# A chunked RWKV-7 recurrence in a hybrid decoder step: chunks of 64 tokens in place of 32, whole-array products, triangles inverted by blocks of 32

## The chip, the cores and the metric

The kernel runs on one core of a Trainium2 chip. The metric is the device time of one execution in microseconds (us). Before the change the median of three runs is 1478.64 us (1477.01 to 1479.61).

## What is computed

One layer of a hybrid decoder for 512 prompt tokens and 8 x 4 sample tokens, all in float32. A pre-RMSNorm and one large input projection (`w_in`, 1024 to 9472 columns) feed three branches (a gMLP gate, an RWKV-7 recurrence, a cross-attention to 256 memory tokens); three branch projections, an output projection and a squared-ReLU MLP follow. The part that is changed is the recurrence, for 16 heads of width 64, over the 512 prompt tokens:

```
def step(S, inp):                      # per token, S is [value, key]
    r_t, w_t, k_t, v_t, a_t, b_t = inp
    sa = einsum('bhij,bhj->bhi', S, a_t)
    S = S * w_t[:, :, None, :] + sa[..., None] * b_t[:, :, None, :] + v_t[..., None] * k_t[:, :, None, :]
    return S, einsum('bhij,bhj->bhi', S, r_t)
```

The kernel does not go token by token. It cuts the prompt into chunks, and inside a chunk the rule is solved by products with a triangular matrix and its inverse; only the state S goes from chunk to chunk.

## The kernel before, in words

**The trunk.** All projections are 128x128 weight tiles against 544 tokens (`trunk`, L490 to L520; the products are at L500). Each weight is split into a high and a low fp32r part (L198 on ScalarE, L211 on VectorE), so a tile costs three products of two column ranges (256 and 288). A "trunk product" below is one of these. The input projection has 74 columns of tiles, 3552 products in all (their inputs are named `hh` and `hl`).

**The streams.** Everything else is a set of generators (`Stream`), which a planner interleaves with the trunk: `build` first runs `body` dry, with a model of each engine's costs (`Model`, L102), notes which stream went next, and then emits the instructions in that order. So each engine's order is fixed, and TensorE, which runs in order, stands still when the next product's input is late. Between the pieces of the other streams the planner puts trunk products; what is left of the input projection after the recurrence's stage runs in the next stage (gate, attention).

**The recurrence's streams** (heads in pairs, two pairs make a group `g`, four groups):
- `prep_pair` (L823): decays, normalised keys, then the Gram products of a pair (L919, L921: 64x64 tiles of the array, 16 chunks), masked by VectorE into `CT`, `A2` (L929 to L935).
- `inv_stream` (L993): for a group, 32 unit triangles of 32x32 are inverted side by side on GpSimd, 30 steps of two instructions (L1007, L1009), with VectorE transposes around (L1002, L1014, L1016), then 64 products of 32x32 tiles (L1021).
- `fill` (L962): the keys are transposed by TensorE (L973, 128 columns to 64 rows) into `Em`, the values by VectorE into `Xe`, `Xo`.
- `chain_stream` (L1044): the serial part. For each of 16 chunks three steps, each a round trip TensorE to ScalarE or VectorE and back: L1063 and L1065 (state and in-chunk inputs), L1079 (the inverse), L1090 and L1092 (the new state). A step is four float32 products in tiles of the array (64x64, 96x64 or 128x64); for TensorE a float32 product is two recorded passes, so a step has eight.
- `out_stream` (L1125), `sample_stream` (L1166): norm and gate of the recurrence's output, and the sample tokens.

In the stage after, `gate_in` (L1413) and `layer_norm` prepare the gate, whose weights `sgw` are loaded and masked (L1469, recorded at L439), and `gate_out` (L1493) uses them.

## Time and profile before

| | us |
|---|---|
| median of three runs | 1478.64 |
| the profiled execution | 1483.1 |
| its span in the profile | 1481.1 |
| TensorE (PE) busy | 1396.5 (94%) |
| VectorE (DVE) busy | 906.7 (61%) |
| ScalarE (ACT) busy | 588.1 (40%) |
| GpSimd (POOL) busy | 396.1 (27%) |

The trace gives each instruction with start, duration, source line, shape and what ended the wait ahead of it. Matmuls are pipelined: a product's own duration (some 0.2 to 0.3 us) is longer than the distance to the next one, so costs on TensorE are read from start to start. In a timeline row `x8` means eight recorded instructions in a row of that kind.

### The profile page before, as it was taken

To read this page: it belongs to the slowest core of one execution; us is meant where nothing else is said; L and a number is where in the kernel's file an instruction comes from. 1 tells how busy PE (TensorE), PEld (TensorE's weight loads), DVE (VectorE), ACT (ScalarE), POOL (GpSimd) and SP (SyncE) were. 2 spreads that over 40 slices of the span, in tenths; PEclk is the share of its full clock that TensorE was granted. 3 is DMA by queue.
4 is the path that set the end of the run, shared out by engine and by line. 5 is a ranking of instruction groups with operands and counts; after the bars stand their busy time and mean duration, and the time that the engine had idled before them with its cause. 6 is when DMAs were issued, how large, how long until landed. Compare 5 with 4: busy or idle time off the path is not lost.

```text
span 1481.1 us, 30854 instructions
## 1 busy us (share of the span) xinstructions
PE 1396.5 (94%) x12340; PEld 1300.1 (88%) x12340; DVE 906.7 (61%) x1570; ACT 588.1 (40%) x1460; POOL 396.1 (27%) x466
## 2 busy tenths in 40 slices
PE   7899979999998899899979999999999999999996
PEld 7799978888878798777879997789999999999996
DVE  5758878848878787686647443344664454444544
ACT  3434326655654466455332222222333423323222
POOL 5320380533047107302234210122100030120213
PEclk9999989989999999899999999999999999999998
DMA  6642312213212323343583677544423222323222
GB/s 219 176 137 84 91 51 78 64 59 100 85 48 84 100 88 98 98 132 116 177 289 113 211 262 245 196 155 134 134 81 95 91 86 86 94 83 95 88 86 82
DMA packets 101888, 177.41 MB, mean 120 GB/s; under 512 B 14929, under 2 KB 28497, under 8 KB 101745
## 3 DMA queue, kind: packets, MB, share of 16 engines
q1 hardware_dynamic: 99904, 172.06, 36.9%
q8 instruction: 97, 1.59, 0.5%
q0 software_dynamic: 640, 2.23, 0.4%
q10 hardware_dynamic: 1200, 1.16, 0.2%
q14 instruction: 47, 0.38, 0.1%
HBM read 147.89 MB, written 27.51 MB: 118 GB/s over the span
## 4 chain that ended last, share of the span: by engine, by line
PE 66%; DVE 11%; POOL 10%; issue 5%; DMA 4%; ACT 3%; SPq 0%; POOLq 0%; DVEq 0%; ACTq 0%
PE pst L500 54%; POOL Xinv L1009 4%; POOL Tt L1007 4%; DVE wlo L211 2%; PE pst L1645 1%; PE pst L1678 1%; PE pst L545 1%; DMA wraw<-memk 1%; PE psc L1079 1%; POOL gn_va L1122 1%; PE psc L1063 1%; PE pst L1021 1%; PE psc L1090 1%; DMA gv<-zv_d 1%; PE pst L1816 1%
## 5 line engine op out<-in xcount | busy, mean ns | idle before, releaser
L211 DVE TENSOR_TENSOR wlo<-wraw,whi 128x512 fp32r<-128x512 f32 x372 | 309.6, 851 | 62.1 <-ACT whi L198 59.9
L198 ACT CAST whi<-wraw 128x512 fp32r<-128x512 f32 x372 | 223.4, 618 | 184.1 <-PE pst L500 103.3
L500 PE MATMUL pst<-hh,whi 128*128 128x256 f32 (+1 forms) x1184 | 258.5, 300 | 5.7 <-DVE y_f L1154 1.9
L500 PE MATMUL pst<-hh,wlo 128*128 128x256 f32 (+1 forms) x1184 | 258.6, 300 | 4.1 <-DVE wlo L211 4.1
L500 PE MATMUL pst<-hl,whi 128*128 128x256 f32 (+1 forms) x1184 | 255.6, 298 | 0.0
L500 PEld LDWEIGHTS pst<-hh,whi 128*128 128x128 f32 x1184 | 192.6, 193 | 13.4 <-issue 2.5
L500 PEld LDWEIGHTS pst<-hh,wlo 128*128 128x128 f32 x1184 | 192.4, 192 | 10.7 <-DVE wlo L211 4.6
L500 PEld LDWEIGHTS pst<-hl,whi 128*128 128x128 f32 x1184 | 193.4, 192 | 5.1 <-issue 1.8
L1784 POOL TENSOR_TENSOR x<-x,dn 128x544 f32<-128x544 f32 x24 | 41.7, 1737 | 293.1 <-DVE dn L1782 293.1
L500 PE MATMUL pst<-gh,whi 128*128 128x256 f32 (+1 forms) x512 | 106.2, 289 | 0.0
L500 PE MATMUL pst<-gl,whi 128*128 128x256 f32 (+1 forms) x512 | 105.5, 287 | 0.0
L500 PE MATMUL pst<-gh,wlo 128*128 128x256 f32 (+1 forms) x512 | 105.2, 288 | 0.0
L1086 ACT COPY YU<-psc 32x64 f32<-32x64 f32 x256 | 51.8, 202 | 81.1 <-DVE Xe L1083 76.9
L1007 POOL TENSOR_TENSOR Tt<-Xinv 128x30 f32<-128x30 f32 (+14 forms) x120 | 66.6, 555 | 64.9 <-DVE Xinv L1002 56.0
L500 PE MATMUL pst<-y_h,whi 128*128 128x256 f32 (+1 forms) x384 | 80.9, 292 | 2.8 <-DVE sp L1499 2.3
L500 PEld LDWEIGHTS pst<-gl,whi 128*128 128x128 f32 x512 | 82.7, 189 | 0.0
L500 PEld LDWEIGHTS pst<-gh,wlo 128*128 128x128 f32 x512 | 81.8, 188 | 0.3 <-DVE wlo L211 0.3
L500 PEld LDWEIGHTS pst<-gh,whi 128*128 128x128 f32 x512 | 81.9, 188 | 0.1
L500 PE MATMUL pst<-y_l,whi 128*128 128x256 f32 (+1 forms) x384 | 80.4, 290 | 0.0
L500 PE MATMUL pst<-y_h,wlo 128*128 128x256 f32 (+1 forms) x384 | 79.9, 290 | 0.0
L500 PE MATMUL pst<-mh,whi 128*128 128x256 f32 (+1 forms) x256 | 65.1, 295 | 10.6 <-ACT whi L198 10.6
L1009 POOL TENSOR_TENSOR Xinv<-Xinv,Tt 128x30 f32<-128x30 f32 (+14 forms) x120 | 72.4, 604 | 9.4
(401 smaller groups left out, 2895.8 us busy)
## 6 DMA issues: line engine op xcount, KB each, us to landing
wraw<-win SPq DMA_DIRECT2D x148, 256.0 KB, 2.9
wraw<-up SPq DMA_DIRECT2D x64, 256.0 KB, 2.9
wraw<-down SPq DMA_DIRECT2D x64, 256.0 KB, 2.9
wraw<-br SPq DMA_DIRECT2D x48, 256.0 KB, 3.6
craw<-ck SPq DMA_DIRECT2D x16, 512.0 KB, 5.4
craw<-cv SPq DMA_DIRECT2D x16, 512.0 KB, 4.4
gz_d<-gzs SPq DMA_DIRECT2D x24, 272.0 KB, 3.6
gt<-gz_d SPq DMA_DIRECT2D x24, 272.0 KB, 2.8
```

Of the source, the lines that this page charges most:

```text
L198: self.nc.scalar.copy(hi, raw)
L211: (self.nc.gpsimd if pool else self.nc.vector).tensor_tensor(lo, raw, hi, op=ALU.subtract)
L500: PE.matmul(ps[:, o:o + n], lhsT=w[:, c], rhs=x[kt][:, s:s + n], start=kt == 0 and i == 0, stop=kt == KT - 1 and i == 2)
L545: PE.matmul(ps[:, o:o + n], lhsT=lhsT, rhs=rhs[:, s:s + n], start=True, stop=True)
L1007: G.tensor_tensor(t3, X[:, j + 1:32, j:j + 1].to_broadcast([128, n, j]), X[:, j:j + 1, 0:j].to_broadcast([128, n, j]), op=ALU.mult)
L1009: G.tensor_tensor(X[:, j + 1:32, 0:j], X[:, j + 1:32, 0:j], t3, op=ALU.add)
L1021: PE.matmul(ps[q:q + 32, m * 32:m * 32 + 32], lhsT=Tt[q:q + 32, m, :], rhs=CT[q:q + 32, m, 0:32], start=True, stop=True, tile_position=(q, q))
L1063: PE.matmul(ps[64:128, pi * 64:pi * 64 + 64], lhsT=Ae[0:96, pi, c, :], rhs=Xe[0:96, pi, c, :], start=True, stop=True, tile_position=(0, 64))
L1079: PE.matmul(ps[q:q + 64, pi * 64:pi * 64 + 64], lhsT=CT[q:q + 64, m, :], rhs=Wt[q:q + 64, pi, :], start=True, stop=True, tile_position=(q, q))
L1086: S.copy(YU[q + 32 * pi:q + 32 * pi + 32, c, :], p3[q:q + 32, pi, :])
L1090: PE.matmul(ps[0:64, pi * 64:pi * 64 + 64], lhsT=Em[64:128, pi, c, :], rhs=Xe[64:128, pi, c, :], start=True, stop=True, tile_position=(64, 0))
L1784: G.tensor_tensor(x1[j], x1[j], t, op=ALU.add)
```

## The change

A chunk has 64 tokens, and there are 8 of them instead of 16 (`CH`, `NCH`). The three steps of a chunk are now products over the whole array (128x64, four of them, in steps one and three; 128x128, two, in step two), without a tile position; of the result one half of the rows is used for each head. The Gram products of a pair are 16 of 64 rows by 128 columns instead of 32 of 64x64, and TensorE's transposes in `fill` are 64 of 128x128 instead of 128 of 128x64. A 64x64 unit triangle is inverted as two 32x32 blocks (the same 30 steps on GpSimd, for 32 blocks side by side) and an off-diagonal block, which takes two sets of 32 products of 32x32, and a third set of 32 products of 64x64 then applies the inverse, in place of one set of 64 products of 32x32. The evacuations of a chunk are spread over ScalarE and VectorE.

```diff
@@ -21,7 +21,7 @@
-CH = 32
+CH = 64
 NCH = TP // CH
...
+    Wts = [sb(rp, [128, 2, 2, 64], f"Wt{i}") for i in range(2)]
...
-            PE.matmul(ps[64:128, o:o + 64], lhsT=BK[0:64, c, :], rhs=A2[0][0:64, pi, c, :],
-                      start=True, stop=True, tile_position=(0, 64))
-            PE.matmul(ps[0:64, o:o + 64], lhsT=BK[64:128, c, :], rhs=A2[1][64:128, pi, c, :],
-                      start=True, stop=True, tile_position=(64, 0))
...
+            ps, sl = yield from take()
+            for i in range(4):
+                for e in range(2):
+                    o = e * 512 + i * 128
+                    PE.matmul(ps[:, o:o + 128], lhsT=BK[64 * e:64 * e + 64, 4 * h + i, :],
+                              rhs=A2[e][64 * e:64 * e + 64, pi, 4 * h + i, :], start=True, stop=True)
+            yield DONE
+            p4 = ps.rearrange("p (e c t) -> p e c t", e=2, t=128)
+            for e in range(2):
+                q, n = 64 * e, 64 - 64 * e
+                m = mk[:, n:n + 128].unsqueeze(1).to_broadcast([128, 4, 128])
+                V.tensor_tensor(CT[q:q + 64, ms, :], p4[64:128, e], m[64:128], op=ALU.mult)
+                V.tensor_tensor(A2[e][n:n + 64, pi, cs, :], p4[0:64, e], m[0:64], op=ALU.mult)
+                yield DONE
...
-            for c in range(c8, c8 + 8):
-                PE.transpose(ps[0:64, (c - c8) * 128:(c - c8) * 128 + 128], BK[:, c, :], ident)
+            for i in range(4):
+                PE.transpose(ps[:, i * 128:i * 128 + 128], BK[:, 4 * half + i, :], ident)
             for n in range(2):
-                V.transpose(Xe[64:96, pi, cs, n * 32:n * 32 + 32],
-                            v[n * 32:n * 32 + 32, tsl].rearrange("p (c t) -> p c t", t=CH))
-                V.transpose(Xo[0:32, pi, cs, n * 32:n * 32 + 32],
-                            v[64 + n * 32:96 + n * 32, tsl].rearrange("p (c t) -> p c t", t=CH))
-            yield DONE
-            p3 = ps[0:64].rearrange("p (c t) -> p c t", t=128)
-            S.copy(Em[0:64, pi, c8:c8 + 8, :], p3[:, :, 64:128])
-            V.tensor_copy(Em[64:128, pi, c8:c8 + 8, :], p3[:, :, 0:64])
+                for th in range(2):
+                    for X, q, r in ((Xe, 64, 0), (Xo, 0, 64)):
+                        V.transpose(X[q + 32 * th:q + 32 * th + 32, pi, cs, n * 32:n * 32 + 32],
+                                    v[r + n * 32:r + n * 32 + 32, tsl].rearrange(
+                                        "p (c t) -> p c t", t=CH)[:, :, 32 * th:32 * th + 32])
+            yield DONE
+            p3 = ps[:, 0:512].rearrange("p (c t) -> p c t", t=128)
+            S.copy(Em[:, pi, cs, 64:128], p3[:, :, 64:128])
+            S.copy(Em[0:64, pi, cs, 0:64], p3[64:128, :, 0:64])
+            V.tensor_copy(Em[64:128, pi, cs, 0:64], p3[0:64, :, 0:64])
...
-            V.transpose(X, CT[:, :, 32:64].rearrange("p m t -> p t m"))
+            for q in (0, 64):
+                V.transpose(X[q:q + 64].rearrange("p t (m h) -> p t m h", h=2),
+                            CT[q:q + 64, :, q:q + 64].rearrange("p m (h t) -> p t m h", h=2))
...
+                G.memset(T4[q:q + 32, :, 1, :], 0.0)
+                for h in range(2):
+                    r = slice(q + 32 * h, q + 32 * h + 32)
+                    G.tensor_copy(CT[r, :, r], TT4[r, :, h, :])
+            yield DONE
+
+            O1 = X[:, 0:16, :]
+            ps, sl = yield from take()
+            for m in range(2 * NCH):
+                for q in (0, 64):
+                    PE.matmul(ps[q + 32:q + 64, m * 32:m * 32 + 32], lhsT=CT[q:q + 32, m, q + 32:q + 64],
+                              rhs=T4[q:q + 32, m, 0, :], start=True, stop=True, tile_position=(q, q + 32))
+            p3 = ps[:, 0:512].rearrange("p (m t) -> p m t", t=32)
+            S.copy(O1[32:64], p3[32:64])
+            V.tensor_copy(O1[96:128], p3[96:128])
+            pt_free(sl)
             yield DONE
             ps, sl = yield from take()
             for m in range(2 * NCH):
                 for q in (32, 96):
-                    PE.matmul(ps[q:q + 32, m * 32:m * 32 + 32], lhsT=Tt[q:q + 32, m, :],
-                              rhs=CT[q:q + 32, m, 0:32], start=True, stop=True, tile_position=(q, q))
-            for pi in range(2):
-                for q in (32, 96):
-                    S.copy(CT[q:q + 32, pi * NCH:pi * NCH + NCH, 0:32],
-                           ps[q:q + 32, pi * 512:pi * 512 + 512].rearrange("p (c t) -> p c t", t=32))
+                    PE.matmul(ps[q:q + 32, m * 32:m * 32 + 32], lhsT=TT4[q:q + 32, m, 1, :],
+                              rhs=O1[q:q + 32, m, :], start=True, stop=True, tile_position=(q, q))
+            p3 = ps[:, 0:512].rearrange("p (m t) -> p m t", t=32)
+            S.copy(T4[32:64, :, 0, :], p3[32:64])
+            V.tensor_copy(T4[96:128, :, 0, :], p3[96:128])
+            pt_free(sl)
+            for q in (0, 64):
+                V.transpose(CT[q:q + 32, :, q + 32:q + 64], T4[q + 32:q + 64, :, 0, :])
+            yield DONE
+            ps, sl = yield from take()
+            for m in range(2 * NCH):
+                for q in (0, 64):
+                    PE.matmul(ps[q:q + 64, m * 64:m * 64 + 64],
+                              lhsT=Tt[q:q + 64, 2 * m:2 * m + 2, :].rearrange("p h t -> p (h t)"),
+                              rhs=CT[q:q + 64, m, 64 - q:128 - q], start=True, stop=True, tile_position=(q, q))
+            p3 = ps.rearrange("p (m t) -> p m t", t=64)
+            S.copy(CT[0:64, :, 64:128], p3[0:64])
+            V.tensor_copy(CT[64:128, :, 0:64], p3[64:128])
...
-                    PE.matmul(ps[64:128, pi * 64:pi * 64 + 64], lhsT=Ae[0:96, pi, c, :], rhs=Xe[0:96, pi, c, :],
-                              start=True, stop=True, tile_position=(0, 64))
-                    PE.matmul(ps[0:64, pi * 64:pi * 64 + 64], lhsT=Ao[:, pi, c, :], rhs=Xo[:, pi, c, :],
-                              start=True, stop=True, tile_position=(0, 0))
-                Wt = sb(rp, [128, 2, 64], "Wt", bufs=2)
-                S.copy(Wt, ps[:, 0:128].rearrange("p (a b) -> p a b", b=64))
+                    for e, (A, X) in enumerate(((Ae, Xe), (Ao, Xo))):
+                        o = pi * 128 + e * 64
+                        PE.matmul(ps[:, o:o + 64], lhsT=A[:, pi, c, :], rhs=X[:, pi, c, :],
+                                  start=True, stop=True)
+                p3 = ps[:, 0:256].rearrange("p (a b) -> p a b", b=128)
+                Wt = Wts[c % 2]
+                S.copy(Wt[0:64, :, 0, :], p3[0:64, :, 0:64])
+                V.tensor_copy(Wt[64:128, :, 1, :], p3[64:128, :, 64:128])
+                S.copy(YU[64:128, :, c, :], p3[64:128, :, 0:64])
+                S.copy(YU[0:64, :, c, :], p3[0:64, :, 64:128])
...
-                    m = pi * NCH + c
-                    for q in (0, 64):
-                        PE.matmul(ps[q:q + 64, pi * 64:pi * 64 + 64], lhsT=CT[q:q + 64, m, :], rhs=Wt[q:q + 64, pi, :],
-                                  start=True, stop=True, tile_position=(q, q))
-                p3 = ps[:, 0:128].rearrange("p (a b) -> p a b", b=64)
-                V.tensor_copy(Xo[32:64, :, c, :], p3[32:64])
-                V.tensor_copy(Xe[96:128, :, c, :], p3[96:128])
-                for pi in range(2):
-                    for q in (0, 64):
-                        S.copy(YU[q + 32 * pi:q + 32 * pi + 32, c, :], p3[q:q + 32, pi, :])
+                    PE.matmul(ps[:, 256 + pi * 128:384 + pi * 128], lhsT=CT[:, pi * NCH + c, :],
+                              rhs=Wt[:, pi].rearrange("p a b -> p (a b)"), start=True, stop=True)
+                p4 = ps[:, 256:512].rearrange("p (a b) -> p a b", b=128)
+                V.tensor_copy(Xe[0:64, :, c, :], p4[0:64, :, 0:64])
+                S.copy(Xo[64:128, :, c, :], p4[64:128, :, 64:128])
+                V.tensor_tensor(YU[64:128, :, c, :], YU[64:128, :, c, :], p4[64:128, :, 0:64], op=ALU.add)
+                V.tensor_tensor(YU[0:64, :, c, :], YU[0:64, :, c, :], p4[0:64, :, 64:128], op=ALU.add)
...
-                    PE.matmul(ps[0:64, pi * 64:pi * 64 + 64], lhsT=Em[64:128, pi, c, :], rhs=Xe[64:128, pi, c, :],
-                              start=True, stop=True, tile_position=(64, 0))
-                    PE.matmul(ps[64:128, pi * 64:pi * 64 + 64], lhsT=Em[0:64, pi, c, :], rhs=Xo[0:64, pi, c, :],
-                              start=True, stop=True, tile_position=(0, 64))
-                p3 = ps[:, 0:128].rearrange("p (a b) -> p a b", b=64)
-                for A, rows in ((Xe, slice(0, 64)), (Xo, slice(64, 128))):
+                    for e, X in enumerate((Xe, Xo)):
+                        o = pi * 128 + e * 64
+                        PE.matmul(ps[:, o:o + 64], lhsT=Em[:, pi, c, :], rhs=X[:, pi, c, :], start=True, stop=True)
...```

Here is TensorE's order around two chain steps of the first group. `psc` is the PSUM tile of a chain step, `Xe` and `Xo` hold state and inputs of the even and the odd head, `AG0e` and `AG0o` the masked Gram products, `CT` the inverse. Before:

```order
L1063 MATMUL psc<-Xe,AG0e 64x64
L1065 MATMUL psc<-Xo,AG0o 64x64
L1063 MATMUL psc<-Xe,AG0e 64x64
L1065 MATMUL psc<-Xo,AG0o 64x64
L500 MATMUL pst<-hh_97,whi 128x256
L500 MATMUL pst<-hh_97,whi 128x288
...
L1079 MATMUL psc<-Wt,CT_1027 64x64 x4
```

The first two steps, with the changed kernel:

```order
L1093 MATMUL psc<-Xe,AG0e 128x64
L1093 MATMUL psc<-Xo,AG0o 128x64
L1093 MATMUL psc<-Xe,AG0e 128x64
L1093 MATMUL psc<-Xo,AG0o 128x64
L500 MATMUL pst<-hl_101,whi 128x256
L500 MATMUL pst<-hl_101,whi 128x288
...
L1108 MATMUL psc<-Wt_1034,CT_1029 128x128 x2
```

In the whole order there were 192 such steps, 135 of which stood alone between trunk products; now there are 96, of which 61 stand alone.

TensorE's order at the first inversion (`Tt` is the inverted block, transposed; `Xinv` the work tile). Before:

```order
L500 MATMUL pst<-hh_93,whi 128x256
L500 MATMUL pst<-hh_93,whi 128x288
L1021 MATMUL pst<-CT_1027,Tt 32x32 x64
L500 MATMUL pst<-hl_101,whi 128x256
```

The same place in the changed kernel:

```order
L500 MATMUL pst<-hh_93,whi 128x288
L1027 MATMUL pst<-Tt,CT_1029 32x32 x32
L500 MATMUL pst<-hl_101,whi 128x256
...
L500 MATMUL pst<-hh_95,wlo 128x288
L1037 MATMUL pst<-Xinv,TT 32x32 x32
L500 MATMUL pst<-hh_96,whi 128x256
...
L500 MATMUL pst<-hh_92,whi 128x288
L1049 MATMUL pst<-CT_1029,Tt 64x64 x32
```

Between the Gram products of pair 1 and the first product of the inversion there were 282 trunk products; now there are 348. Between the first product of `gate_in` and the first of `gate_out`, in the stage after, there were 410; now there are 294. From `gate_out` on, TensorE's order is the same in both kernels.

## Rows read from the trace of the kernel before

**Rows 1.** The page, part 1: busy time of each engine.
```profile
PE 1396.5 (94%) x12340; PEld 1300.1 (88%) x12340; DVE 906.7 (61%) x1570; ACT 588.1 (40%) x1460; POOL 396.1 (27%) x466
```
**Rows 2.** Windows: stretch, length, busy us by engine, granted clock, DMA share, GB/s.
```profile
82.00:755.00 673.00, 633.05 (x6380) 567.16 (x6380) 501.69 (x983) 337.88 (x992) 231.41 (x311) 0.96 0.31 95
```
**Rows 3.** Waits of TensorE from 105 to 755: us in total, times, longest.
```profile
PE psc L1090 <- DVE Xe L1083: 11.5, 10, 3.1
PE pst L1021 <- DVE Tt L1014: 7.1, 1, 7.1
PE psc L1063 <- DVE Xe L1098: 3.3, 3, 1.3
```
**Rows 4.** Timeline of TensorE around a chain step: start, duration.
```profile
247.04 0.41 PE L500 MATMUL pst<-hl,whi 128*128 128x256 f32 x2
247.29 0.41 PE L500 MATMUL pst<-hh,wlo 128*128 128x256 f32 x2
247.63 0.27 PE L1063 MATMUL psc<-Xe,AG0e 96*64 96x64 f32 x1
...
247.86 0.22 PE L1065 MATMUL psc<-Xo,AG0o 128*64 128x64 f32 x1
...
248.37 0.41 PE L500 MATMUL pst<-hl,whi 128*128 128x256 f32 x2
```
**Rows 5.** Groups by line, TensorE: the second chain step's recorded passes.
```profile
L1079 PE MATMUL psc<-Wt,CT 64*64 64x64 f32 x512 | 28.9, 232 | 0.0
```
**Rows 6.** Timeline of TensorE: whole-array passes of 2 columns, then trunk.
```profile
231.61 1.17 PE L858 MATMUL pst<-bones,t_x 128*128 128x2 f32 x10
232.64 0.50 PE L500 MATMUL pst<-hl,whi 128*128 128x256 f32 x2
232.97 0.41 PE L500 MATMUL pst<-hh,wlo 128*128 128x256 f32 x2
```
**Rows 7.** Timeline of TensorE: whole-array passes of 128 and 32 columns, then trunk.
```profile
831.92 1.05 PE L1493 MATMUL pst<-sgw,vn 128*128 128x128 f32 x8
832.81 0.31 PE L1494 MATMUL pst<-sgs,vn 128*128 128x32 f32 x2
832.95 0.49 PE L500 MATMUL pst<-y_l,whi 128*128 128x256 f32 x2
```
**Rows 8.** Groups by line: the trunk's weight loads (PEld).
```profile
L500 PEld LDWEIGHTS pst<-hh,whi 128*128 128x128 f32 x1184 | 192.6, 193 | 13.4 <-issue 2.5
```
**Rows 9.** Timeline of TensorE: two products in tiles of 64 rows.
```profile
229.06 0.38 PE L845 MATMUL pst<-la,wa 64*128 64x256 f32 x1
229.07 0.38 PE L846 MATMUL pst<-la,wa 64*128 64x256 f32 x1
229.28 0.40 PE L845 MATMUL pst<-la,wa 64*128 64x288 f32 x1
```
**Rows 10.** Timeline of TensorE: the Gram products of pair 0, first pass and trunk after.
```profile
124.19 0.27 PE L919 MATMUL pst<-AG0e,BK 64*64 64x64 f32 x1
...
126.21 0.52 PE L500 MATMUL pst<-hl,whi 128*128 128x256 f32 x2
```
**Rows 11.** Timeline of TensorE: eight transposes of `fill`, then trunk.
```profile
180.18 1.03 PE L973 MATMUL pst<-ident,BK 128*64 128x128 f32 x8
180.97 0.49 PE L500 MATMUL pst<-hh,whi 128*128 128x256 f32 x2
```
**Rows 12.** Timeline of TensorE: products of the first inversion, and of the third.
```profile
220.04 3.62 PE L1021 MATMUL pst<-CT,Tt 32*32 32x32 f32 x128 [7.14 <-DVE Tt L1014]
...
489.37 2.21 PE L1021 MATMUL pst<-CT,Tt 32*32 32x32 f32 x128
```
**Rows 13.** Groups by line, VectorE: the transpose ahead of an inversion.
```profile
L1002 DVE STREAM_TRANSPOSE Xinv<-CT 128x1024 f32<-128x1024 f32 x4 | 7.9, 1980 | 0.1
```
**Rows 14.** Timeline: the gate's weights masked on GpSimd, and their first product.
```profile
816.42 1.10 POOL L439 TENSOR_SCALAR_AFFINE_SELECT sgw<-sgw 128x1024 f32<-128x1024 f32 x1 [6.33 <-issue]
...
829.55 1.05 PE L1493 MATMUL pst<-sgw,vn 128*128 128x128 f32 x8
```

More of the change, by code (lines that the diff above doesn't have):

```diff
@@ L705, in body @@
     vb_d = dp.tile([8, 128, TP], F32, name="vb_d")
-    for i in range(2):
-        G.memset(AG[i][1][32:64], 0.0)
-    G.memset(Xo[32:64], 0.0)
     G.memset(PP[:, :, 0:1], 1.0)
```

97 lines of the change are left out of this document (45 added, 52 removed).

## The prediction, made before the changed kernel was run

> **What bounds the kernel now.** I read the busy times first, then windows, then the waits, then single steps on the timeline. The reader is to see in the first that TensorE is busy for 94% of the span, and no other engine for more than 61% [rows 1]. The windows show where the other 6% lie: in the recurrence's stage (82 to 755 us) TensorE is busy for 633 of 673 us, at a granted clock of 0.96 [rows 2]. So even the stage with the serial chain in it is filled, because trunk products stand between the chain's steps. The trunk does not run dry there: input projection is left over and runs in the next stage. Hence a shorter chain by itself is worth nothing here. What counts is TensorE's time on the small products, the breaks that they make in the trunk, and the waits that stop the in-order queue. The waits [rows 3] are few: 14.8 us for the chain's steps (11.5 and 3.3) and 7.1 us, once, for the first inversion.
>
> A small step costs more than its products. Trunk pairs follow each other in 0.25 us (247.04, 247.29). Around L1063 and L1065 the pair at 247.29 is followed by the second pair after it at 248.37: 1.08 us where two pairs take 0.50 [rows 4]. A chain step standing alone thus costs 0.58 us; the same count on a step of L1079 and of L1090 gives the same. Its eight passes start within 0.23 us (247.63 to 247.86), which I take as their price; 0.35 us is the break: 0.09 us late into the tiles, the rest on the way out of them.
>
> **The chain's products.** Before, 64 chunks of three steps make 192 steps (the 512 passes of the second step alone are 64 x 8 [rows 5]). The 135 that stand alone cost 78 us; the other 57 share a break with other small products, and I take 0.38 us for them (estimate: 0.23 us and part of a break), 22 us. Together 100 us; 111 if all stood alone.
>
> Afterwards a step is over the whole array, and no row shows one of 64 columns. Two bounds: ten whole-array passes of 2 columns take 1.03 us from the first to the trunk that follows (231.61 to 232.64 [rows 6]), and ten of 128 and 32 columns take 1.03 us as well (831.92 to 832.95 [rows 7]). Both ends say 0.103 us a pass, so I take that. The break is small: the first trunk pair takes 0.33 us instead of 0.25 (232.64 to 232.97). Steps one and three have four products, eight passes, 0.82 us; step two has two products of 128 columns, four passes, 0.41 us. 32 chunks cost 32 x 2.05 = 66 us, and 61 breaks of 0.08 us add 5: 71 us. **Minus 29 us** (minus 40 if all old steps stood alone).
>
> So it is not that the whole array is quicker: one pass for one pass, tiles are (0.03 against 0.10 us). A chunk of 64 tokens replaces six interruptions by three, and these cost little each. The Trainium skill (TensorEngine Tiling (Array Packing), Theoretical Speedup) speaks against this change: it says that products with a dimension of 64 or less gain up to twofold by tiles. By that rule alone, which counts products and no break, the chain would go from 192 x 0.23 = 44 us to 66 us, plus 22 in place of minus 29, and the kernel would come to 1498 us. The trace does not follow it: a step's price from start to start [rows 4] is more than twice its products.
>
> **The other products of the stage.** *Transposes in fill:* eight take 0.79 us [rows 11]; now four do the work, 0.1 us each, 16 times: minus 6 us. *Gram products:* 64 passes take 2.0 us (124.19 to 126.21 [rows 10]) and the break 0.2 more. Now a pair has two sets of 16 passes, 64 rows by 128 columns. Two such products in different rows of the array run side by side (start 0.01 us apart, the next 0.21 us later for 256 columns [rows 9]); half of the columns make 0.1 us for a pair of passes, 0.85 us a set and 0.35 us for its break, 2.4 us in all. Eight times 0.2 us: plus 2 us. If they did not run side by side it would be plus 15.
> *Inversion:* 128 passes of 32x32 take 3.6 us where the clock is low and 2.2 us later [rows 12], plus one break. Now two sets of 64 such passes (1.1 to 1.8 us each), one of 64 passes in 64x64 tiles (1.9 us at the 0.03 us of a chain pass) and three breaks of 0.35 us: 5.2 to 6.6 us instead of 2.6 to 4.0. Four times 2.6 us: plus 11 us.
> VectorE and ScalarE move about the same number of elements in this stage, in part in smaller pieces; VectorE is busy 502 of 673 us there [rows 2], so there is cover, and I cost them at nothing as such; where they come late shows as a wait.
>
> **The waits.** The chain's 14.8 us came in 13 stalls over 192 steps; with half as many steps I take half: minus 7 us (between 0 and minus 12). For the first inversion, TensorE's queue reaches its product 7.1 us too early [rows 3, 12]. Behind the Gram products of pair 1 there are now 348 trunk products instead of 282, 66 x 0.124 = 8.2 us more of work; the transposes and Gram products in that stretch are about 1.5 us shorter. The inversion's path gets longer by one VectorE transpose: it goes in two halves of 64 rows now, and I count each at the full 1.98 us [rows 13], since the row length is the same. GpSimd's 30 steps stay as they are. 7.1 + 2 + 1.5 - 8.2 leaves some 2 us: minus 5 us. The copies of the diagonal blocks that GpSimd gets in addition come after the first set of products; 42 trunk products and two sets (some 8 us) stand ahead of the third, which needs them, and cover them.
>
> **The next stage.** From the first gate transposes to the first gate product TensorE now has 116 trunk products fewer, 14.4 us. That first product started at 829.55; the weights it needs were masked at 817.5 (816.42 + 1.10 [rows 14]), 12.0 us ahead. So the cover is just used up: plus 2 us (0 to 8, as the normalisation ahead of it is itself partly paced by the trunk). After it the order is unchanged, and so is the cost.
>
> **The sum.** -29 - 6 + 2 + 11 - 7 - 5 + 2 = -32 us. It is made against the profiled execution, 1483.1 us (span 1481.1): 1451 us. That execution is 4.5 us above the median of the runs, 1478.64, so for the median I say **1447 us**.
>
> **The rivals.**
> *The chain's waits stay.* Half as many steps, but each moves twice the data: in step one two copies of 64 rows feed the next product instead of one of 128, and in step three VectorE comes after two additions for the output. If all 21.9 us of these waits stay, 12 us of the gain go: 1459 us; with the Gram products one after the other as well (13 us), 1472 us. For it: the largest item of the waits is VectorE being late [rows 3]. Against: 10 to 16 trunk products (1.2 to 2 us) stand between two steps in most places of the new order.
> *A whole-array step pays the same break.* If 0.35 us of each interruption comes from leaving the trunk, and not from the tiles, then 61 breaks cost 16 us more: 1463 us. Against: the two whole-array rows show 0.08 us [rows 6, 7].
> *Whole-array passes wait for their weights (slower).* Every new pass has its own weights. The trunk's weight loads last 0.193 us [rows 8], and are hidden under products of 256 and 288 columns; with 64 columns there is less to hide them under. If a load and a pass went one after the other, at about 0.19 us a pass, the chain's 640 passes would cost 122 us and breaks, 127 instead of 71: the sum turns to plus 24 us, 1503 us. It decides from about 0.15 us a pass (32 us more over 640 passes). Against: ten passes with ten weights in 1.03 us [rows 6]. For it: no row shows 64 columns out of fresh chain data.
>
> **How the numbers follow.** My forecast has 0.70, the waits that stay 0.15, the equal break 0.07, the weight loads with what the tiling rule says (slower) 0.08. The range reaches on the high side to the waits with the Gram products one after the other, 1472 us; on the low side the chain at minus 40 us, 5 us more of waits gone and a granted clock somewhat above 0.96 (of some 27 us that it can cost at most, 4% of 673 us, a few) make 1428 us. A measurement of this kernel can tell 0.2%, 3 us, from no change. Faster by more than that: the forecast and most of the first two rivals, 0.88; within: 0.04, where those two come together; slower: 0.08.
>
> **What would show it.** Right: eight passes of L1093 within 0.85 us and four of L1108 within 0.45 us, with the next trunk pair at most 0.1 us late; TensorE's small products some 22 us shorter in the stage; waits on VectorE for chain steps under 10 us, and a wait of 0 to 4 us at the first L1027. Wrong: passes of 0.15 us and more, single waits of several us at L1027, L1037 or L1049 in every group, or several us of standstill ahead of the first gate product.

## The result and the profile after

The changed kernel takes 1491.96 us (median of 4 runs, 1489.53 to 1493.13); the kernel before took 1477.83 us beside it (1472.68 to 1479.61). The ratio is 1.0099, with an interval of 1.0070 to 1.0128: slower by one per cent, where 2% faster was forecast. The profiled execution has a span of 1491.4 us, 10.3 us more than before.

The page of the changed kernel, its span and part 1:
```profile
span 1491.4 us, 28541 instructions
...
PE 1387.3 (93%) x11380; PEld 1318.7 (88%) x11380; DVE 923.6 (62%) x1622; ACT 520.4 (35%) x1152; POOL 413.4 (28%) x489
```
Against [rows 1], TensorE is busy for 9.2 us less, and yet the span grew. Span less busy time is TensorE's standstill: 1481.1 - 1396.5 = 84.6 us before, 1491.4 - 1387.3 = 104.1 us now, 19.5 us more. VectorE has 16.9 us more to do.

Windows of the changed kernel, with the columns of [rows 2], over the stretch shown there and over one that takes in the whole chunk stage of both kernels (before it ends at 755 us, now at 779):
```profile
82.00:755.00 673.00, 617.56 (x5405) 580.86 (x5404) 502.99 (x1017) 267.84 (x681) 240.07 (x320) 0.95 0.28 91
...
80.00:800.00 720.00, 653.49 (x5631) 613.96 (x5632) 528.84 (x1057) 283.58 (x714) 252.48 (x342) 0.94 0.32 101
```
and the longer stretch in the kernel before:
```profile
80.00:800.00 720.00, 671.64 (x6637) 602.45 (x6638) 533.41 (x1037) 356.75 (x1036) 249.42 (x334) 0.96 0.33 103
```
The standstill of this stretch went from 48.4 to 66.5 us, and the granted clock from 0.96 to 0.94: of the 19.5 us of new standstill 18.1 lie in this stage. VectorE's busy time does not show why: from 82 to 755 us it is 501.7 us before and 503.0 now.

TensorE's waits in the changed kernel, 82 to 800 us (total, times, longest):
```profile
PE psc L1120 <- DVE Xe L1111: 7.4, 3, 5.0
...
PE pst L500 <- DVE wlo L211: 5.4, 5, 2.1
PE pst L1298 <- DVE so L1303: 3.5, 2, 1.9
PE pst L500 <- DVE t_L L874: 3.5, 2, 3.2
PE pst L920 <- DVE t_vb L908: 3.4, 1, 3.4
...
PE pst L842 <- DVE Em L976: 3.0, 1, 3.0
PE psc L1093 <- DVE Xe L1126: 2.3, 4, 1.2
PE pst L500 <- DVE AG1o L928: 2.2, 1, 2.2
```
The waits of [rows 3] answer to the two `psc` lines: the chain's fell from 14.8 to 9.7 us, and the one of 7.1 us for the first inversion is gone. In their place stands a long list of small ones, at the Gram products (L920), the preparation's products (L842, L500), the samples (L1298). Most of them are for VectorE. With all rows of this view added up, from 80 to 800 us, TensorE waited 33.7 us for VectorE before and 50.6 us now; without the chain's steps and the first inversion it is 11.8 us before and 40.9 now.

A chain step standing alone, timeline of TensorE:
```profile
303.07 0.41 PE L500 MATMUL pst<-hl,whi 128*128 128x256 f32 x2
303.31 0.33 PE L1120 MATMUL psc<-Xe,Em 128*128 128x64 f32 x2
...
304.12 0.50 PE L500 MATMUL pst<-hh,wlo 128*128 128x256 f32 x2
304.45 0.42 PE L500 MATMUL pst<-hh,whi 128*128 128x256 f32 x2
304.71 0.41 PE L500 MATMUL pst<-hl,whi 128*128 128x256 f32 x2
```
Eight passes take 0.81 us (303.31 to 304.12) and the trunk resumes 0.08 us late (0.33 where 0.25 is usual): the step is as cheap as forecast.

VectorE's groups that prepare the chunks or bring out their results (Y), called preparation from here on, in the kernel before (busy us, mean ns, idle before); the one of L1002 stands in [rows 13]:
```profile
L1142 DVE STREAM_TRANSPOSE y_f<-YU 32x512 f32<-32x512 f32 x16 | 11.3, 704 | 0.2
L1140 DVE STREAM_TRANSPOSE y_f<-YU 32x512 f32<-32x512 f32 x16 | 11.2, 702 | 12.6 <-POOL YU L1123 8.9 <-DMA yb_d<-y_f 3.4
L975 DVE STREAM_TRANSPOSE Xe<-t_v 32x256 f32<-32x256 f32 x32 | 13.9, 435 | 0.6
L977 DVE STREAM_TRANSPOSE Xo<-t_v 32x256 f32<-32x256 f32 x32 | 13.9, 434 | 0.4
L1014 DVE STREAM_TRANSPOSE Tt<-Xinv 128x1024 f32<-128x1024 f32 x4 | 8.3, 2068 | 3.6 <-POOL Xinv L1009 3.6
L1016 DVE STREAM_TRANSPOSE CT<-Xinv 128x1024 f32<-128x1024 f32 x4 | 7.8, 1960 | 0.1
```
and in the changed kernel:
```profile
L1171 DVE STREAM_TRANSPOSE y_f<-YU 32x256 f32<-32x256 f32 x64 | 27.9, 436 | 13.9 <-POOL YU L1151 11.5 <-DMA yb_d<-y_f 1.4
L969 DVE STREAM_TRANSPOSE Xe<-t_v 32x128 f32<-32x128 f32 x64 | 19.4, 303 | 1.0
L969 DVE STREAM_TRANSPOSE Xo<-t_v 32x128 f32<-32x128 f32 x64 | 19.3, 302 | 0.9
L998 DVE STREAM_TRANSPOSE Xinv<-CT 64x1024 f32<-64x1024 f32 x8 | 16.1, 2013 | 0.1
L1011 DVE STREAM_TRANSPOSE Tt<-Xinv 128x1024 f32<-128x1024 f32 x4 | 8.4, 2103 | 2.2 <-POOL Xinv L1006 2.2
L1013 DVE STREAM_TRANSPOSE TT<-Xinv 128x1024 f32<-128x1024 f32 x4 | 8.1, 2013 | 0.0
L1044 DVE STREAM_TRANSPOSE CT<-Tt 32x512 f32<-32x512 f32 x8 | 5.6, 703 | 0.2
L1054 DVE COPY CT<-pst 64x1024 f32<-64x1024 f32 x4 | 4.9, 1227 | 8.8 <-ACT CT L1053 8.8
L1031 DVE COPY Xinv<-pst 32x512 f32<-32x512 f32 x4 | 2.8, 696 | 2.9 <-ACT Xinv L1030 2.8
```
Here is what the small change of VectorE's total hides. Transposes out of Y: 22.5 to 27.9 us. Transposes of v into X: 27.8 to 38.7. The inversion: 8.3 + 7.9 + 7.8 = 24.0 before, 48.7 now (the six groups above from L998 on, with another copy of 2.8 at L1041). Together **41 us more of preparation**: 16 us are copies and transposes that the kernel before did not have (L1031, L1041, L1044, L1054), 25 us come from the same elements in smaller pieces. In exchange the chain's own copies and additions (L1082, L1083, L1098 and the few of its first steps and its end before; L1098, L1111, L1113, L1114, L1126 and the same few now) fell from 73.9 to 54.9 us and those of Em (L982, now L976) from 10.9 to 6.7.

One of the new waits as it arises, timeline of VectorE and TensorE around 440 us:
```profile
436.24 3.96 DVE L998 STREAM_TRANSPOSE Xinv<-CT 64x1024 f32<-64x1024 f32 x2
440.23 0.30 DVE L969 STREAM_TRANSPOSE Xe<-t_v 32x128 f32<-32x128 f32 x1
...
442.44 0.30 DVE L969 STREAM_TRANSPOSE Xo<-t_v 32x128 f32<-32x128 f32 x1
442.78 0.28 DVE L1111 COPY Xe<-psc 64x128 f32<-64x128 f32 x1
443.12 0.69 PE L1120 MATMUL psc<-Xe,Em 128*128 128x64 f32 x2 [4.98 <-DVE Xe L1111]
...
452.12 0.66 PE L500 MATMUL pst<-hh,whi 128*128 128x256 f32 x2
452.57 0.66 PE L500 MATMUL pst<-hl,whi 128*128 128x256 f32 x2
...
455.46 0.41 PE L500 MATMUL pst<-hh,wlo 128*128 128x256 f32 x2
455.71 0.41 PE L500 MATMUL pst<-hh,whi 128*128 128x256 f32 x2
```
Two transposes for the next inversion and eight for the next fill stand ahead of a copy of 0.28 us that the chain needs; TensorE stands still for 4.98 us. What follows is the second part of the loss: trunk pairs come every 0.45 us at 452 us and every 0.25 us at 455. Windows of that place say why (granted clock: third figure from the end):
```profile
441.00:454.00 13.00, 10.88 (x43) 9.34 (x44) 8.10 (x24) 6.80 (x16) 11.35 (x22) 0.50 0.09 21
454.00:470.00 16.00, 14.37 (x117) 13.97 (x117) 13.49 (x29) 6.52 (x16) 13.55 (x16) 1.00 0.17 56
```
A granted clock of 0.50 is 1.2 GHz, 1.00 is 2.4 GHz. From 430 to 438 us it was 1.00; inside the standstill (438.1 to 443.1) it fell, it stayed at 1.2 GHz until 454 us, and then it was 2.4 GHz again. The mean clock of the whole span gives the time at half rate, 2 x (1 - clock) x span: 74 us before (0.975), 98 us after (0.967).

### The profile page after: what moved, and what is told of

It is laid out like the page before. It is cut to its first block, busy times and chain, and to the rows that moved or that the text cites. A ratio compares the mean times of both kernels' runs of the same rounds, so it can differ in the third digit from the quotient of the medians.

```text
span 1491.4 us, 28541 instructions
## 1 busy us (share of the span) xinstructions
PE 1387.3 (93%) x11380; PEld 1318.7 (88%) x11380; DVE 923.6 (62%) x1622; ACT 520.4 (35%) x1152; POOL 413.4 (28%) x489
## 5 line engine op out<-in xcount | busy, mean ns | idle before, releaser
L211 DVE TENSOR_TENSOR wlo<-wraw,whi 128x512 fp32r<-128x512 f32 x372 | 320.6, 880 | 45.7 <-ACT whi L198 43.7
L500 PE MATMUL pst<-hh,whi 128*128 128x256 f32 (+1 forms) x1184 | 259.3, 301 | 9.3 <-DVE t_L L874 3.5
L500 PE MATMUL pst<-hh,wlo 128*128 128x256 f32 (+1 forms) x1184 | 258.1, 300 | 7.7 <-DVE wlo L211 7.6
L500 PE MATMUL pst<-hl,whi 128*128 128x256 f32 (+1 forms) x1184 | 257.3, 299 | 0.0
L500 PEld LDWEIGHTS pst<-hh,whi 128*128 128x128 f32 x1184 | 196.1, 195 | 13.2 <-DVE t_L L874 3.4
L500 PEld LDWEIGHTS pst<-hh,wlo 128*128 128x128 f32 x1184 | 195.4, 195 | 12.1 <-DVE wlo L211 9.4
L500 PEld LDWEIGHTS pst<-hl,whi 128*128 128x128 f32 x1184 | 197.2, 195 | 4.2 <-issue 2.5
L500 PE MATMUL pst<-gh,whi 128*128 128x256 f32 (+1 forms) x512 | 106.2, 289 | 0.0
L500 PE MATMUL pst<-gl,whi 128*128 128x256 f32 (+1 forms) x512 | 105.5, 287 | 0.0
L500 PE MATMUL pst<-gh,wlo 128*128 128x256 f32 (+1 forms) x512 | 105.2, 287 | 0.0
L500 PE MATMUL pst<-y_h,whi 128*128 128x256 f32 (+1 forms) x384 | 81.2, 293 | 3.2 <-DVE sp L1528 2.6
L500 PEld LDWEIGHTS pst<-gl,whi 128*128 128x128 f32 x512 | 82.7, 189 | 0.0
L500 PEld LDWEIGHTS pst<-gh,whi 128*128 128x128 f32 x512 | 81.9, 188 | 0.1
L500 PEld LDWEIGHTS pst<-gh,wlo 128*128 128x128 f32 x512 | 81.7, 188 | 0.3 <-DVE wlo L211 0.3
L500 PE MATMUL pst<-y_l,whi 128*128 128x256 f32 (+1 forms) x384 | 80.6, 291 | 0.0
L500 PE MATMUL pst<-y_h,wlo 128*128 128x256 f32 (+1 forms) x384 | 80.1, 291 | 0.0
L1006 POOL TENSOR_TENSOR Xinv<-Xinv,Tt 128x30 f32<-128x30 f32 (+14 forms) x120 | 73.3, 611 | 9.4
L500 PE MATMUL pst<-mh,whi 128*128 128x256 f32 (+1 forms) x256 | 65.1, 295 | 10.4 <-ACT whi L198 10.3
L1789 DVE TENSOR_TENSOR ff_r<-ff_r,pst 128x544 f32<-128x544 f32 x32 | 23.1, 721 | 81.5 <-ACT ff_r L1788 81.5
```

The lines of the kernel that those rows point to most:

```text
L211: (self.nc.gpsimd if pool else self.nc.vector).tensor_tensor(lo, raw, hi, op=ALU.subtract)
L500: PE.matmul(ps[:, o:o + n], lhsT=w[:, c], rhs=x[kt][:, s:s + n], start=kt == 0 and i == 0, stop=kt == KT - 1 and i == 2)
L1006: G.tensor_tensor(X[:, j + 1:32, 0:j], X[:, j + 1:32, 0:j], t3, op=ALU.add)
L1789: V.tensor_tensor(r, r, ps[:, 256:800], op=ALU.mult)
```

## The experiments

Two ideas stood at the start: **theory A**, that the plan's prices are wrong (a block transpose on VectorE takes 2.0 us where the plan counts 1.1; a whole-array product takes twice the plan's time), so that it hands TensorE products before VectorE is ready; and **theory B**, that VectorE is now what TensorE waits for, because TensorE's work shrank and VectorE's did not. The table has all runs: median and ratio to the kernel before, and of the profiled execution the span, TensorE's busy time, the standstill (span less busy) and the mean clock. The last four come from one execution of each kernel, which lies up to 7 us from its median.

| kernel | median us | ratio, interval | span | busy | still | clock |
|---|---|---|---|---|---|---|
| before | 1477.8 | | 1481.1 | 1396.5 | 84.6 | 0.975 |
| b_prices | 1477.3 | 1.0006 (0.9987 to 1.0026) | 1472.8 | 1385.4 | 87.4 | 0.984 |
| b_lopool | 1479.0 | 1.0022 (0.9999 to 1.0045) | 1473.1 | 1387.7 | 85.4 | 0.984 |
| b_cal | 1481.4 | 1.0032 (1.0011 to 1.0053) | 1486.2 | 1399.3 | 86.9 | 0.968 |
| b_nudge_up | 1474.2 | 0.9983 (0.9960 to 1.0006) | 1476.1 | 1389.0 | 87.1 | 0.981 |
| b_vfree | 1466.0 | 0.9923 (0.9893 to 0.9953) | 1459.6 | 1385.2 | 74.4 | 0.983 |
| b_xcopy | 1470.7 | 0.9958 (0.9938 to 0.9978) | 1471.0 | 1392.8 | 78.2 | 0.977 |
| b_vmore | 1504.8 | 1.0193 (1.0152 to 1.0234) | 1505.0 | 1402.1 | 102.9 | 0.968 |
| after | 1492.0 | 1.0099 (1.0070 to 1.0128) | 1491.4 | 1387.3 | 104.1 | 0.967 |
| a_prices | 1469.8 | 0.9956 (0.9933 to 0.9979) | 1467.9 | 1372.7 | 95.2 | 0.978 |
| a_lopool | 1479.7 | 1.0030 (1.0010 to 1.0049) | 1473.1 | 1376.2 | 96.9 | 0.977 |
| a_dve | 1495.8 | 1.0135 (1.0102 to 1.0168) | 1494.4 | 1387.4 | 107.0 | 0.967 |
| a_pe | 1490.2 | 1.0112 (1.0065 to 1.0160) | 1488.6 | 1385.0 | 103.6 | 0.972 |
| a_cal | 1482.3 | 1.0037 (1.0017 to 1.0056) | 1474.4 | 1371.3 | 103.1 | 0.972 |
| a_both | 1491.6 | 1.0101 (1.0072 to 1.0130) | 1489.2 | 1387.5 | 101.7 | 0.967 |
| a_nudge_up | 1482.7 | 1.0045 (1.0026 to 1.0063) | 1481.8 | 1380.1 | 101.7 | 0.970 |
| a_nudge_down | 1492.5 | 1.0107 (1.0066 to 1.0149) | 1492.4 | 1384.2 | 108.2 | 0.969 |
| a_xcopy | 1473.7 | 0.9982 (0.9964 to 1.0001) | 1473.8 | 1379.1 | 94.7 | 0.975 |
| a_vfree | 1473.1 | 0.9971 (0.9953 to 0.9989) | 1468.4 | 1377.8 | 90.6 | 0.971 |
| a_vlean | 1461.8 | 0.9897 (0.9868 to 0.9926) | 1460.1 | 1370.2 | 89.9 | 0.980 |

**First round: prices, and VectorE's load.** Both prices put right in the plan, in the changed kernel and in the one before:
```diff
+            if r > 0.5e-3 and "tile_position" not in k:
+                t = max(t, 0.104 if name == "transpose" else 0.208)
...
+            if name == "transpose":
+                t = 0.07 + n * (1.9e-3 if n >= 1024 else 1.25e-3)
```


> The changed kernel with two prices of its planner corrected from the traces: a strided VectorE transpose of 1024 elements 2.0 us instead of 1.1 (512 elements 0.71, 256 0.39), and a whole-array float32 product at least 0.21 us instead of 0.11 for 64 columns. Only the order of the instructions changes. Theory A (TensorE waits for a VectorE that the plan puts too early): standstill before the gate's stage falls from 62 to about 45 us, time falls by 10 to 20 us against the changed kernel, to 1472 to 1482. Theory B (VectorE has too much work whatever the order): within 5 us of the changed kernel. Theory C (the products themselves are dearer than forecast): within 5 us, standstill unchanged.

> The kernel before with the same two prices. Theory A: little to correct there, 0 to 8 us faster than before. Theory B and C: within 4 us of before.

And the load alone: low parts of weights in the stage are moved from VectorE to GpSimd. In the traces 72 are moved in the changed kernel and 77 in the one before, not the 39 and 42 of the expectations; VectorE's busy time falls by 25.6 us (923.6 to 898.0) and 21.3 us (906.7 to 885.4):
```diff
-            self.plan.lo.append(POOL_LO and max(m.free["g"], m.start) + POOL_LO < max(m.free["v"], m.start))
+            self.plan.lo.append(32 <= self.nlo < 180 and max(m.free["g"], m.start) + 0.5 < max(m.free["v"], m.start))
```


> The changed kernel with some of the trunk's low-part subtractions of the input projection (39 of 148) moved from VectorE to GpSimd, where the plan finds GpSimd free sooner. Theory B: VectorE's load falls by some 30 us, the waits for it by 10 us or more, time falls by 10 to 15 us. Theory A: 0 to 8 us. Theory C: no change.

> The kernel before with 42 of the same subtractions moved to GpSimd. Theory B: falls by less than the changed kernel does, 3 to 8 us. Theory A and C: within 4 us of before.

The prices took 22 us off the changed kernel and nothing off the other. That looked like theory A, with some of B in the 12 us of a_lopool; b_lopool gained nothing (1479.0), where theory B had 3 to 8 us.

**Second round: which price.** a_dve has the last two lines of the edit of a_prices, a_pe the first two; a_cal and b_cal have a fuller set of measured prices, among them those of products in tiles of the array and of going into and out of them:
```diff
+            elif "tile_position" in k:
+                t, kind = 0.034 if n <= 32 else 0.06 if n <= 64 else 0.1, 1
...
+            if kind != self.kind:
+                t += 0.1 if kind else 0.25
...
+            t = 0.15 + n / 960.0
```

> The changed kernel; in the plan's prices only those of VectorE's 32x32 block transposes are put right (0.07 us + 1.9 ns a column from 1024 columns up, 1.25 ns below; before, they were priced like a copy), so only the order of the work changes. With both prices put right the changed kernel took 1469.8 us against 1492.0. Theory A1 (the plan takes VectorE to be ready too early, since the strided X transposes take twice what it counts): this edit alone gives nearly all of it, 1468 to 1476, and TensorE's idle time in the chunk stage falls below 58 us. Rival A2 (it is TensorE's whole-array fp32 products that the plan counts at half their time): nothing here, 1486 to 1495. Rival A3 (any other order would do as well, since the order as it stands is an unlucky one): both single edits land near 1475 to 1480.

> The changed kernel; in the plan's prices only TensorE's whole-array fp32 products (at least 0.208 us) and transposes (0.104 us) are put right, VectorE's stay. Theory A1: little, 1484 to 1494. Rival A2: 1468 to 1476. Rival A3: 1475 to 1480, as with the other edit.

> The changed kernel with a fuller set of prices in the plan: VectorE's transposes and whole-array products as in the run with both put right, beside them products on tiles at 0.034, 0.06 and 0.1 us, products on 64 rows at 0.85 ns a column, 0.1 us into and 0.25 us out of tile mode, and 0.15 us of fixed time for VectorE and ScalarE. If wrong prices are what the changed kernel lost (theory A), this is no slower than 1469.8, 1458 to 1470, and the idle time of TensorE in the chunk stage falls towards 45 us. If the order was unlucky and prices don't matter as such (rival A3), it lands anywhere from 1465 to 1490.

> The kernel before with the same fuller set of prices. Its chain has the breaks that hold slack, and the two prices alone did nothing to it (1477.3). Theory A: again 1472 to 1480, so that the changed kernel is faster by 8 us or more once both are planned by measured prices. Rival: the prices of tile mode matter most where its breaks are most, and this one gains as much as the other, 1455 to 1468.

Theory A, in this form, fell. Neither half does anything (1495.8 and 1490.2, where both together gave 1469.8), and the fuller set of prices made a worse order than the two prices did (1482.3). The times look like draws from a lot: any edit of a price gives another order, and the changed kernel takes what that order happens to cost.

**Third round: the order held still.** Here the plan is made as before, and only the instruction that is issued in its place differs, so that TensorE's order is the same to the product. In a_xcopy the transposes of the inversion become copies:
```diff
-                V.transpose(X[q:q + 64].rearrange("p t (m h) -> p t m h", h=2),
+                (V.transpose if dry else V.tensor_copy)(
+                    X[q:q + 64].rearrange("p t (m h) -> p t m h", h=2),
```
and the same at L1011 and L1013. In a_vfree and b_vfree every second low part is a copy on ScalarE:
```diff
+        if not self.dry and 32 <= self.nlo < 180 and self.nlo % 2:
+            self.nc.scalar.copy(lo, raw)
+        else:
```
a_both joins the edits of a_prices and a_lopool.

> The changed kernel with every engine's order kept to the instruction; only VectorE's four 32x32 block transposes of X per inversion (2.0 us each) run as plain copies of the same tiles, which is what the plan priced them at. The inverses are left out thereby. Theory A1 (these transposes make VectorE later than planned): TensorE's idle time in the chunk stage falls by the 4 x 4 x 0.9 us that VectorE gains or more, from 62 us to below 45, and the time to 1470 or less. Rival A3 (the two single prices did nothing, so it is where the order happens to put the waits): less than 6 us, 1485 to 1494.

> The changed kernel with every engine's order kept; of the 148 low parts of weights in the chunk stage that VectorE subtracts (0.69 us each), every second one is a plain copy on ScalarE instead (so the low parts are left out there): VectorE has 51 of its 503 us less to do, TensorE the same. Theory B (TensorE got shorter and VectorE did not, so that VectorE is what TensorE now waits for): idle time falls from 62 to 35 us or less, the half-rate time with it, and the time by 25 us or more, to 1467 or less. Rival A3: 1480 to 1495.

> The kernel before with the same edit, order kept. Theory B: its TensorE is behind VectorE less often, so it gains less than half of what the changed kernel does, 1465 to 1477. Rival: it gains as much, so that VectorE bounds both alike and the difference lies elsewhere.

> The changed kernel with both prices put right in the plan and, besides, some of the chunk stage's low parts on GpSimd where the plan sees VectorE more than 0.5 us later than GpSimd. Each alone gave 1469.8 and 1479.7. If prices and VectorE's load are two separate costs (theories A and B), the gains add: 1457 to 1467. If each was no more than another order (rival A3), anything from 1468 to 1492.

The group that a_xcopy shortens, and its page, part 1:
```profile
L998 DVE COPY Xinv<-CT 64x1024 f32<-64x1024 f32 x8 | 8.8, 1100 | 0.1
...
PE 1379.1 (94%) x11380; PEld 1310.8 (89%) x11380; DVE 909.9 (62%) x1622; ACT 520.5 (35%) x1152; POOL 412.2 (28%) x489
```
13.7 us less on VectorE (923.6 to 909.9) are 18 us less of time: TensorE does wait for what stands behind these transposes. Of the 18 us, 9.4 are standstill, which is less than was expected, and the rest goes with the clock (0.967 to 0.975): TensorE's same products keep it busy for 8.2 us less. The 53 us of VectorE that a_vfree saves are worth hardly more (19 us), and b_vfree's only 12. So it is not VectorE's busy time as such that costs, which is against theory B as it was put: low parts cost 0.26 us of standstill for 1 us of VectorE (13.5 / 52.6), the inversion's transposes 0.69 (9.4 / 13.7). The 0.26 may be too low: in a_vfree ScalarE has 38 us more to do (520.4 to 558.8), and what that costs was not taken apart. And a_both, 1491.6, fits the draws: two edits that gave 22 and 12 us give nothing together.

**Fourth round: is it this order, or the change?** Two plans of the changed kernel and one of the other, in which VectorE's fixed part counts 0.01 us more or less, and, as b_xcopy, the edit of a_xcopy in the kernel before, at its L1002, L1014 and L1016. The nudge upwards:
```diff
-            t = 0.07 + n / 960.0
+            t = 0.08 + n / 960.0
```


> The kernel before with every engine's order kept to the instruction; VectorE's three block transposes of X per inversion run as plain copies of the same tiles (the inverses are left out thereby). In the changed kernel the same edit took 15 us off VectorE and 18 us off the time. Theory S (the chain before holds slack in its breaks, which the change took away, so that only the changed kernel waits for a late VectorE): less than 5 us, 1472 to 1478. Rival: both are as sensitive, 11 us of VectorE give 8 to 14 us here, 1462 to 1469, and the extra waits of the changed kernel come from its VectorE work alone.

> The changed kernel; VectorE's fixed part in the plan 0.08 us instead of 0.07, which means nothing for the work but gives another order. If the 1492 us belongs to the change, 1486 to 1496. If the order decides by itself (rival A3), anywhere from 1468 to 1496, with TensorE's idle and half-rate time going along: 10 us less of idle time and 30 us less at half rate make about 20 us.

> As the other nudge, with 0.06 us. If the time belongs to the change: 1486 to 1496. Rival A3: anywhere from 1468 to 1496, and the two nudges differ by more than 5 us from each other or from the changed kernel.

> The kernel before with the same nudge, 0.08 us. Its four orders so far took 1477 to 1481. Theory S: again 1473 to 1482, since slack makes it indifferent to the order. Rival: it scatters like the changed kernel, by 10 us or more.

The nudges came 10 us apart, so the order alone is worth that much. But there is now a sample: nine orders of the changed kernel's work took 1469.8 to 1495.8 us (median 1490.2), five of the kernel before 1474.2 to 1481.4 (median 1477.8). The two overlap, but seven of the nine are slower than all five, and the changed kernel as it stands is 2 us above the median of its orders. So the result is no unlucky draw. And the standstill is the plainest difference: 84.6 to 87.4 us in all five of the one, 95.2 to 108.2 in all nine of the other. b_xcopy lies between its two expectations, 7 us of time for 9.4 us of transposes (24.0 to 14.6). Its standstill fell by 6.4 us, 0.68 for 1 us of transposes, which is as much as in a_xcopy (9.4 us for 13.9).

**Fifth round: the preparation, both ways.** a_vlean has the edit of a_xcopy, and beside it copies of 64 rows in place of the transposes of v into X, and copies of 512 columns in place of those out of Y; b_vmore repeats transposes in the kernel before. Of a_vlean:
```diff
-            for n in range(2):
+            if not dry:
+                for n in range(2):
+                    for X, q, r in ((Xe, 64, 0), (Xo, 0, 64)):
+                        V.tensor_copy(X[q:q + 64, pi, cs, n * 32:n * 32 + 32],
...
-                    for th in range(2):
+                    if not dry:
+                        for r, q in ((0, 64), (64, 0)):
+                            V.tensor_copy(yt[r + hf * 32:r + hf * 32 + 32, :, :], YU[q:q + 32, pi, :, :])
```
Of b_vmore:
```diff
-            V.transpose(Tt.rearrange("p m t -> p t m"), X.rearrange("p t s -> p s t"))
+            for _ in range(1 if dry else 3):
+                V.transpose(Tt.rearrange("p m t -> p t m"), X.rearrange("p t s -> p s t"))
...
-            for n in range(2):
+            for n in range(2) if dry else (0, 0, 1):
```


> The changed kernel with the order of TensorE, ScalarE, GpSimd and the DMA queue kept. VectorE's preparation is cut to about the size that it had before: X's transposes in the inversion are plain copies, the 128 transposes of v into X are 64 copies of twice the rows, the 64 transposes of Y are 32 copies of twice the columns (inverses and transposes are left out thereby); together some 41 us less. The inversion's part alone took the standstill of TensorE from 104 to 95 us and the time from 1492 to 1474. Theory V (the added preparation on VectorE is what TensorE waits for): standstill 80 to 90 us, as before the change, and 1455 to 1466 us. Rival S (the shorter chain has no slack left, whatever VectorE does): it stays above 92 us, 1468 to 1476 us.

> The kernel before with the order of TensorE, ScalarE, GpSimd and the DMA queue kept; VectorE does one of the inversion's transposes three times instead of once (2 x 2.07 us in each of four inversions) and half of the transposes of v into X twice: 30 us more of preparation. Theory V: standstill from 85 to 98 us or more and 1490 us or more. Rival S (its chain's breaks hold the slack): below 90 us, 1476 to 1483 us.

Page of a_vlean, part 1:
```profile
PE 1370.2 (94%) x11380; PEld 1303.4 (89%) x11380; DVE 897.7 (61%) x1526; ACT 520.1 (36%) x1152; POOL 413.4 (28%) x489
```
Page of b_vmore, part 1:
```profile
PE 1402.1 (93%) x12340; PEld 1305.0 (87%) x12340; DVE 938.7 (62%) x1610; ACT 588.1 (39%) x1460; POOL 393.9 (26%) x466
```
and its largest waits from 80 to 800 us (its lines stand one further down than those of [rows 3]):
```profile
PE psc L1091 <- DVE Xe L1084: 20.8, 15, 5.1
PE pst L500 <- DVE wlo L211: 8.8, 4, 7.1
PE pst L1022 <- DVE Tt L1015: 8.8, 1, 8.8
PE psc L1064 <- DVE Xe L1099: 5.9, 4, 2.2
```
Both landed where theory V put them. a_vlean cut VectorE by 25.9 us (not 41: the copies into X take 0.56 us each and come to 36.1 us in place of 38.7); the standstill fell by 14.2 us, to 89.9, and the time by 30.2, which makes it 1% faster than the kernel before. In b_vmore 32.0 us more of the same work make the kernel before stand still for 102.9 us, as much as the changed one, and 28 us slower. Per us of preparation that is 0.55 and 0.57 us of standstill. Rival S, that the old chain has slack, is out: the kernel before is as sensitive. Its waits for a late VectorE just land elsewhere, at the chain's steps (20.8 us where there were 11.5). TensorE's waits for VectorE from 80 to 800 us, all rows added up, go along: 33.7 us in the kernel before and 54.6 in b_vmore, 50.6 in the changed one and 36.5 in a_vlean.

## Why the prediction was wrong

**The sum that the runs give.** Over all runs but a_cal (which lies 9 us lower, and why was not looked into; with it the numbers below change by 1 us), TensorE's busy time in the profile is a constant plus 0.34 us for each us at half rate (least squares, within 5 us for each run): 1369 us for the kernel before, 1352 for the changed one. So TensorE's work itself fell by 17 us. The standstill grew by 19.5 us, and 24 us more at half rate cost 8 by this fit. Together 10.5 us; the span grew by 10.3.

**Right: TensorE's work.** Forecast were -29 - 6 + 2 + 11 = -22 us, measured is -17. The chain's steps of eight passes take 0.81 us where they stand alone, those of four 0.36 (247.19 to 247.55; forecast 0.82 and 0.41), with the trunk 0.08 us late. The Gram products run side by side: a set of 16 standing alone takes 1.09 us (117.45 to 118.54) and the trunk resumes 0.10 late, where 0.85 and 0.35 were counted. The first two sets of an inversion take 1.13 us each at the full clock and the third 2.0 (1.1 and 1.9). The 5 us between -22 and -17 were not traced to one term. The prediction's other signs of being right came true as well; none of them looked at VectorE's added work, so they could come true while the time went the other way.

**Right: the rival on weight loads falls.** The rule of the Trainium skill (TensorEngine Tiling (Array Packing), Theoretical Speedup) and the serial weight loads gave 1498 and 1503 us, and the time came out near them, but not for their reason: passes of 64 columns take 0.10 us (eight in 0.81). The trace does not follow the rule here, since TensorE's work became less without the tiles. That rival had the sign, and neither its place nor its price.

**Right: the next stage, the first inversion, the chain's waits.** No wait stands at the first L1027 (0 to 4 us forecast). The chain's waits for VectorE are 9.7 us, under the 10 that were named, though not the 7.4 of the sum. In the next stage the first gate product comes 60 us after the first gate transposes (779.1 to 839.5) instead of 74 (755.3 to 829.6), 14 us earlier as worked out, though the traces count 104 trunk products fewer there (398 and 294) and not 116; the waits there did not grow (7.1 us at the gate's transposes before, 6.7 now, and 0.3 ahead of the first gate product).

**Wrong: "VectorE and ScalarE move about the same number of elements in this stage, in part in smaller pieces ... so there is cover, and I cost them at nothing as such."** This is the step that failed. The pieces were counted by elements, not by rows of the trace, although the prediction itself priced a half of 64 rows at the full 1.98 us, for the path of the first inversion alone. None of its rivals has this term. A transpose of 32 x 128 takes 0.30 us where one of 32 x 256 takes 0.435; one of 64 x 1024 takes as long as one of 128 x 1024; and the off-diagonal blocks bring copies and transposes that the kernel before did not have. That is 41 us, on an engine that was busy for 75% of the stage, while ScalarE, put at nothing as well, got 68 us less to do (588.1 to 520.4). At 0.55 to 0.69 us of standstill for each us of such work it makes 23 to 28 us; less 23 us of relief in the chain and Em at the 0.2 to 0.26 us of the low parts (0.2 from b_vfree, 10.2 us for 53.8; an estimate: what the chain's copies are worth was not measured by itself), 17 to 24 us. Measured is 19.5. That preparation on VectorE costs standstill is shown by the runs of the fifth round; that it makes up the whole 19.5 rests on this estimate.

**Wrong: the waits, minus 12.** The waits that were looked at did fall, by 12 us (21.9 to 9.7). But the sum took it that waits exist only where the trace of before shows them. Outside of these, from 80 to 800 us, TensorE stood still for 26.5 us before (48.4 - 21.9) and for 56.8 now (66.5 - 9.7). The new ones are 4 us or less each, and no single one would have been called a bound.

**Wrong: the clock as it was.** The forecast left it out of the sum, and its range let it make the time shorter only. By the fit it costs 8 us. The half-rate stretch shown above goes with a single standstill of 5 us; half-rate time does not go by the sum of the standstills, since of two kernels with the same order of TensorE a_vfree stood still for 90.6 us at 0.971 and a_xcopy for 94.7 at 0.975 (over their ten executions 0.969 to 0.976 and 0.975 to 0.982).

**Not settled.** Why the standstill of the changed kernel scatters over orders by 13 us and that of the kernel before by 3. Whether the 41 us of preparation can be had for less with the inverses in place was not tried; the runs with copies leave them out. Nor was it tried to give the new copies to ScalarE. And why a copy of 64 x 128 into X takes 0.56 us in a_vlean, where a transpose of 32 x 128 takes 0.30, is open.

One version that computes the same is faster than both kernels: a_prices, 1469.8 us, 0.9956 (0.9933 to 0.9979) of the kernel before. It is the best of nine orders, and a_cal and a_both, which have its prices among others and took 1482.3 and 1491.6 us, speak against these prices as the reason.

## What to carry to other kernels

When one engine is full and another three quarters full, the second one's work is priced like the first one's: list its groups before and after, by rows and not by elements, because here each half of an instruction, on half of the rows, cost as much as the whole (2.01 and 1.98 us). Slack must be sought where the work is needed next, not in the share of the stage. And where a planner sets the order, time several plans that are alike to it before a difference of 1% is put down to an edit: here the same work took from 1470 to 1496 us.

## What was not expected of the hardware

A block transpose of 32 x 32 on VectorE with 1024 elements in a row takes 2.01 us on 64 rows and 1.96 to 2.10 us on 128, and as a plain copy 1.05 to 1.10 us in most places (1.40 and 1.56 us for the one into `Tt`, in a_xcopy and b_xcopy). At 0.30 us for 128 elements in a row, 0.435 for 256 and 0.70 for 512 it has some 0.17 us of fixed time (an estimate: 0.30 less half of 0.70 - 0.435).

A standstill of TensorE can cost more than itself. Around the 4.98 us above the clock fell to 1.2 GHz for 13 us, 11 of them behind the standstill, in which trunk pairs took 0.45 us instead of 0.25; over the runs of the fit a us at half rate goes with 0.34 us more of TensorE's busy time.
